# Up phase of a hybrid transformer layer: operand sums on VectorE alone, another priority scope, and the stores of u on ScalarE's queue

## The chip, the cores and the metric

The kernel runs on one core of one Trainium2 chip. The metric is the device time of one execution in microseconds. A core has five engines with an instruction queue each: PE (TensorE, matmuls), DVE (VectorE), ACT (ScalarE), POOL (GpSimd) and SP (SyncE, which here only issues DMAs). Each engine takes its instructions in order. ACT can issue DMAs as well. Matmul results go to PSUM, which has eight banks; DVE and ACT read them out of there.

## What is computed

The reference is one step of one layer for a prompt of 1024 rows and a sample of 8 x 16 rows, in fp32: an attention branch with a forget gate, a gated-delta branch, a merge of both, and a channel mixer. The change touches the channel mixer alone:

```
def channel_mixer(x, pre_g, post_g, w_up, w_down):
    h = rmsnorm(x, pre_g)
    u = jnp.square(jax.nn.relu(h @ w_up))
    return x + rmsnorm(u @ w_down, post_g)
```

`w_up` is 1024 x 4096 and `w_down` 4096 x 1024. Prompt and sample are worked on together: 1152 rows of h, nine tiles of 128.

## The kernel before

Each fp32 matmul is made of three: a value is split into a high and a low part (`split`, L325: ACT casts the high part, L326; DVE subtracts it to get the low part, L327), and high x high, high x low and low x high are added up in PSUM (`mm3`, L147, the matmul itself at L150). h lies transposed in SBUF as `hhi` and `hlo` (the profile calls them mhi and mlo in this phase).

The up phase (L1238 to L1360) computes u transposed, 32 row tiles of 128 features. Its first four row tiles are plain products (`gemm_t`, three groups of 384 columns each; `evu` does Relu and Square on ACT, L1280 and L1281, and stores to the DRAM tensor `u_d`, L1283). Beside them `h_sums` makes the operands `TT[0..3]` (th) from h: for each pair of column tiles two differences made by `diff` (x and y on POOL, L1252 and L1253, their sum on DVE, L1254), two by `rest` (both steps on DVE, L1259 and L1260), and a split of each into th. In all 20 POOL operations, 16 of 128x512 and 4 of 128x256.

The other 28 row tiles are done in 14 pairs by Winograd's form of Strassen's scheme: seven products in place of eight, each of sums of weight blocks with sums of h blocks. `w_ops` is a generator of the weight operands. For a pair it loads four blocks (`wr`, L1308, on SP), makes four sums (`add`, L1295, on POOL, tile `ws`) and splits the seven operands into `wh` and `wl`. The loop takes them three ahead (`ahead`). Each product has two column groups c, 320 and 256 wide, of 12 matmuls each, and each group takes one of eight PSUM banks in turn. Results are read out by ACT (product 0, a copy, L1357) or DVE (all others, `plus`, an addition to a running sum, L1347), into `s` tiles, of which there are 14 (and 4 `s1`). Four times a pair a row tile is finished in each column group: Relu (L1351), Square (L1352) and the store to `u_d` (L1353), eight stores a pair.

The down phase (from L1362) loads row tiles of u back (`ur`, L1400) and blocks of `w_down` (`raw`, L1406), both on SP, splits them into us and wd, and multiplies. A load of `gpost` (L1410) stands near its start in SP's queue.

The order of instructions in each queue is not the order of the code. A framework places them before the run, by the priority at which they were written (`tc.high_priority(n)` puts what is written inside its scope n places ahead) and by its model of costs. It also puts in the waits: a tile's buffer is reused when its readers are done, and each DMA signals on one of eight completion semaphores in turn, so that it first waits for the one before on the same semaphore. In `w_ops` the `yield` stands inside the scope of priority 50: while the generator rests there, the scope is still open, and what the consumer writes then (matmuls, evictions, stores) is written inside it.

Of the kernel before, what the change touches and what calls it, by code (L numbers as in the profile page):

```python
# [12 lines left out]
ALU = mybir.AluOpType  # L13
# [41 lines left out]
E0 = 4  # L55
XB = 1
LOW = 100000
HI = 200
KBB = 3
RB = 2  # L60
# [5 lines left out]
def tile_step(ctx, tc, x_prompt, x_sample, cache_k, cache_v, cache_logf, state_gdn, state_conv,  # L66
# [4 lines left out]
    V, A, G, S, T = nc.vector, nc.scalar, nc.gpsimd, nc.sync, nc.tensor  # L71
# [83 lines left out]
    hhi = ph.tile([P, NTT, KT, P], F32R, name="hhi")  # L155
    hlo = ph.tile([P, NTT, KT, P], F32R, name="hlo")
# [912 lines left out]
    with tc.tile_pool(name="fp", bufs=1, reuse_waits="tile") as fp:  # L1069
# [15 lines left out]
        for p in range(NP_):  # L1085
            q, k, v2, vn, qkn = nxt
            oT = fp.tile([P, NPR], F32, tag="oT", bufs=2, name=nm("oT"))
            for hh in range(2):
# [5 lines left out]
                for s in range(4):  # L1094
                    pr = fox_scores(fp, s, *qk)
# [14 lines left out]
    hhi = ph.tile([P, NTT, KT, P], F32R, name="mhi")  # L1110
    hlo = ph.tile([P, NTT, KT, P], F32R, name="mlo")
# [119 lines left out]
    u_d = dr.tile([DFF // P, P, 2, TH], F32, name="u_d")  # L1231
# [6 lines left out]
    with tc.tile_pool(name="up", bufs=1, reuse_waits="tile") as up:  # L1238
        def h_sums(t0, t1):

            n = t1 - t0

            def B(h, i, j):
                return f(h[:, t0:t1, 4 * i:4 * i + 4, 64 * j:64 * j + 64])

            def tmp():
                z = up.tile([P, 4, P], F32, tag="ws", bufs=4, name=nm("ws"))
                return z.rearrange("p k (t n) -> p (k t n)", t=2).rearrange("p (t k n) -> p t k n", t=2, k=4)[:, :n]

            def diff(a, b):  # L1250
                x, y = tmp(), tmp()
                G.tensor_tensor(x, B(hhi, *a), B(hhi, *b), ALU.subtract)  # L1252
                G.tensor_tensor(y, B(hlo, *a), B(hlo, *b), ALU.subtract)  # L1253
                V.tensor_tensor(x, x, y, ALU.add)  # L1254
                return x

            def rest(a, x):
                y = tmp()
                V.tensor_tensor(y, B(hhi, *a), x, ALU.subtract)  # L1259
                V.tensor_tensor(y, y, B(hlo, *a), ALU.add)  # L1260
                return y

            def out(i, x):
                split(x, *(z[:, :, 64 * t0:64 * t1].rearrange("p k (t n) -> p t k n", n=64) for z in TT[i]))
            t1_ = diff((0, 1), (0, 0))
            out(0, t1_)
            t2_ = rest((1, 1), t1_)
            out(1, t2_)
            out(2, diff((1, 1), (0, 1)))
            out(3, rest((1, 0), t2_))  # L1270

# [5 lines left out]
        for ft in range(N0):  # L1277
            def evu(c, acc, ft=ft):
                r, u = piece("s", 14, CH), piece("s", 14, CH)
                A.activation(r, acc, AF.Relu)  # L1280
                A.activation(u.rearrange("p (h t n) -> p t h n", h=2, n=64),  # L1281
                             r.rearrange("p (t h n) -> p t h n", h=2, n=64), AF.Square)
                S.dma_start(u_d[ft, :, :, 192 * c:192 * c + 192], u.rearrange("p (h n) -> p h n", h=2))  # L1283
            gemm_t(weights(halves(w_up[0], ft * P)), hhi, hlo, KT, evu, tag=("mm", NMM[0]))
            for t in ((0, 2), (4,), (6, 8), ())[ft]:
                h_sums(t, min(t + 2, NTT))
# [4 lines left out]
        def w_ops():  # L1291

            def add(x, y, op):
                z = up.tile([P, 4, P], F32, tag="ws", bufs=4, name=nm("ws"))
                G.tensor_tensor(z, x, y, op)  # L1295
                return z

            def parts(x):
                h, l = (wps_["w"].tile([P, 4, P], F32R, tag="w" + z, bufs=WBUFS["w"][1], name=nm("w" + z)) for z in "hl")
                split(x, h, l)  # L1300
                return h, l
            for pr in range(N0 // 2, DFF // P // 2):
                a = {}
                with tc.high_priority(200):
                    for i in range(2):
                        for j, src in enumerate(halves(w_up[0], (2 * pr + i) * P)):
                            a[i, j] = wps_["w"].tile([P, 4, P], F32, tag="wr", bufs=WBUFS["w"][0], name=nm("wr"))
                            S.dma_start(a[i, j], src.rearrange("(k p) n -> p k n", p=P))  # L1308
                with tc.high_priority(50):
                    yield parts(a[0, 0])  # L1310
                    s1 = add(a[1, 0], a[1, 1], ALU.add)
                    s2 = add(s1, a[0, 0], ALU.subtract)
                    yield parts(s2)
                    yield parts(add(a[0, 0], a[1, 0], ALU.subtract))
                    yield parts(a[1, 1])
                    yield parts(s1)
                    yield parts(a[0, 1])
                    yield parts(add(a[0, 1], s2, ALU.subtract))

        def hop(i, j):  # L1320
            return lambda k, t0, t1: [z[:, t0:t1, 4 * i + k, 64 * j:64 * j + 64] for z in (hhi, hlo)]
# [7 lines left out]
        for pr in range(N0 // 2, DFF // P // 2):  # L1329
            sm = [[], []]  # L1330
            for i, b in enumerate(prods):
                while len(ahead) < 3:
                    nx = next(made, None)
                    if nx is None:
                        break
                    ahead.append(nx)
                wh, wl = ahead.pop(0)
                for c, (t0, t1) in enumerate(GR):
                    n = 64 * (t1 - t0)
                    o = pt("mm", 8)[:, :n]  # L1340
                    mm3(o, [p3 for k in range(4) for hi, lo in (b(k, t0, t1),) for p3 in (
                        (wh[:, k], hi), (wh[:, k], lo), (wl[:, k], hi))])

                    def plus(x, r=None):
                        if r is None:
                            r = piece("s", 14, n)
                        V.tensor_tensor(r, o, x, ALU.add)  # L1347
                        return r

                    def done(row, half, r):  # L1350
                        A.activation(r, r, AF.Relu)  # L1351
                        A.activation(r, r, AF.Square)  # L1352
                        S.dma_start(u_d[2 * pr + row, :, half, 64 * t0:64 * t1], r)  # L1353
                    z = sm[c]
                    if i == 0:
                        r = piece("s1", 4, n)
                        A.copy(r, o)  # L1357
                        z.append(r)
                    elif i == 1:
                        z.append(plus(z[0]))  # L1360
                    elif i == 2:
                        z.append(plus(z[1]))  # L1362
                    elif i == 3:
                        done(1, 0, plus(z[2]))
                    elif i == 4:
                        plus(z[1], z[1])
                        done(1, 1, plus(z[2], z[2]))
                    elif i == 5:
                        done(0, 0, plus(z[0]))
                    else:  # L1370
                        done(0, 1, plus(z[1], z[1]))
# [22 lines left out]
    for blk in range(nb):  # L1394
        us, wd = uset[blk % 2], dset[blk % 2]
        for i in range(FB):
            ft = blk * FB + i
# [89 lines left out]
```

## Time and profile before

| | us |
|---|---|
| time, median of 3 runs | 2034.62 (2031.67 to 2039.93) |
| the profiled execution | 2027.51 |
| its span (first to last instruction) | 2025.7 |
| PE busy in 1200.0 to 1602.4 (end of the up phase's matmuls) | 390.98 of 402.40 |
| DVE, ACT, POOL busy there | 225.84, 193.16, 104.40 |
| PE busy from 1602.4 to the end (down phase) | 401.74 of 423.30 |

All times in the following are microseconds from the span's start, in the profiled execution. An engine's busy time counts only computing instructions; an idle stretch is followed by what ended it. A line such as L327 is a line of the kernel; a helper like `split` has the same line for every tile, so the tile's name tells which operation it is. `SPq` and `ACTq` are the queues in which these engines issue DMAs. The rows that the prediction rests on stand in it.

### The profile page before, as it was taken

What the parts mean: (1) busy time and instruction counts of PE and PEld (TensorE: products, weight loads), DVE (VectorE), ACT (ScalarE), POOL (GpSimd) and SP (SyncE); (2) the same over time, 40 slices, a digit from 0 to 9 for tenths busy, and PEclk for the clock granted to TensorE, in tenths of its full rate; (3) what the DMA queues carried; (4) which work ended last, traced back from release to release, by engine and by line L of the source; (5) the groups of instructions that cost most, each with busy time, mean ns of one, the idle gap of its engine ahead of it and who ended that gap; (6) DMA issues with size and microseconds to landing.
All of it is one profiled execution on the core that took longest, in us unless ns stands there. A gap on an engine that the chain in (4) does not pass through costs nothing.

```text
span 2025.7 us, 31077 instructions
## 1 busy us (share of the span) xinstructions
PE 1923.0 (95%) x11228; PEld 1725.9 (85%) x11228; DVE 1159.7 (57%) x2627; ACT 925.7 (46%) x2160; POOL 338.7 (17%) x433
## 2 busy tenths in 40 slices
PE   7989999898999999999989999899999799999998
PEld 6979898798898878778989789899999678888886
DVE  6357577775765476776644469745454444444437
ACT  5433474654737475665543444455454451111112
POOL 1141332513312200000012004422222000000000
PEclk9999999999999999999999999999999899999999
DMA  6142424224243543432643631333232452322203
GB/s 192 44 101 67 100 67 113 69 76 130 54 133 109 172 155 101 141 107 80 203 137 106 203 108 45 94 99 104 83 110 67 153 186 90 98 92 93 87 16 146
DMA packets 240310, 219.33 MB, mean 108 GB/s; under 512 B 53628, under 2 KB 213176, under 8 KB 240156
## 3 DMA queue, kind: packets, MB, share of 16 engines
q1 hardware_dynamic: 225888, 198.09, 33.1%
q10 hardware_dynamic: 14268, 19.25, 2.7%
q8 instruction: 89, 1.46, 0.3%
q14 instruction: 65, 0.53, 0.1%
HBM read 155.54 MB, written 61.74 MB: 107 GB/s over the span
## 4 chain that ended last, share of the span: by engine, by line
PE 75%; DVE 8%; DMA 7%; ACT 5%; issue 3%; POOL 2%; SPq 1%; DVEq 0%; POOLq 0%; ACTq 0%
PE mm L150 44%; PE mf L150 13%; PE pc L1011 2%; PE pa L150 1%; DMA be<-rows_o 1%; PE pc L150 1%; DVE th L327 1%; PE pe L150 1%; DVE xs L610 1%; DMA out_dram<-kst 1%; PE pb L150 1%; PE pd L150 1%; DMA wor<-in_w_out_dram 1%; PE mm L1040 1%; PE mm L1061 1%
## 5 line engine op out<-in xcount | busy, mean ns | idle before, releaser
L150 PE MATMUL mm<-wd,us 128*128 128x512 f32 x1728 | 401.7, 394 | 11.7 <-ACT wd L326 11.7
L150 PEld LDWEIGHTS mm<-wd,us 128*128 128x128 f32 x1728 | 325.7, 189 | 87.5 <-ACT wd L326 13.3
L150 PE MATMUL mf<-hhi,wlo 128*128 128x384 f32 x744 | 262.0, 352 | 3.2 <-DVE wlo L327 3.2
L150 PE MATMUL mf<-hhi,whi 128*128 128x384 f32 x744 | 260.9, 351 | 1.8 <-ACT gst L211 1.8
L150 PE MATMUL mf<-hlo,whi 128*128 128x384 f32 x744 | 261.4, 351 | 0.0
L150 PE MATMUL mm<-th,wh 128*128 128x256 f32 (+1 forms) x896 | 178.1, 295 | 4.5 <-ACT wh L326 3.6
L1435 DVE TENSOR_TENSOR yacc<-mm,yacc 128x512 f32<-128x512 f32 x126 | 86.2, 688 | 128.8 <-PE mm L150 128.6
L1347 DVE TENSOR_TENSOR s<-mm,s 128x320 f32<-128x320 f32 (+1 forms) x196 | 85.2, 454 | 108.3 <-PE mm L150 107.0
L150 PEld LDWEIGHTS mm<-th,wh 128*128 128x128 f32 x896 | 142.6, 189 | 5.1 <-ACT wh L326 3.8
L150 PEld LDWEIGHTS mf<-hhi,wlo 128*128 128x128 f32 x744 | 141.5, 190 | 4.4 <-DVE wlo L327 4.1
L150 PEld LDWEIGHTS mf<-hhi,whi 128*128 128x128 f32 x744 | 141.4, 190 | 2.4 <-ACT gst L211 2.1
L150 PEld LDWEIGHTS mf<-hlo,whi 128*128 128x128 f32 x744 | 141.3, 190 | 0.6
L150 PE MATMUL mm<-th,wl 128*128 128x320 f32 (+1 forms) x448 | 126.3, 296 | 0.7 <-DVE wl L327 0.7
L326 ACT CAST wd<-raw 128x512 fp32r<-128x512 f32 x64 | 38.3, 619 | 187.1 <-DVE yacc L1435 80.0
L327 DVE TENSOR_TENSOR wlo<-raw,whi 128x512 fp32r<-128x512 f32 x110 | 76.6, 698 | 69.5 <-ACT whi L326 68.7
L150 PE MATMUL mm<-mhi,wh 128*128 128x320 f32 (+1 forms) x336 | 100.5, 299 | 6.2 <-DVE s L1347 4.5
L150 PE MATMUL mm<-hhi,whi 128*128 128x384 f32 x288 | 103.7, 360 | 2.7 <-ACT whi L326 2.1
L150 PE MATMUL mm<-hhi,wlo 128*128 128x384 f32 x288 | 100.5, 349 | 2.1 <-DVE wlo L327 2.1
L150 PE MATMUL mm<-hlo,whi 128*128 128x384 f32 x288 | 101.9, 354 | 0.0
L326 ACT CAST whi<-raw 128x512 fp32r<-128x512 f32 x110 | 68.0, 619 | 68.1 <-PE mf L150 31.0
L150 PE MATMUL mm<-mhi,wl 128*128 128x320 f32 (+1 forms) x336 | 98.9, 294 | 0.0
L150 PE MATMUL mm<-mlo,wh 128*128 128x320 f32 (+1 forms) x336 | 98.9, 294 | 0.0
(494 smaller groups left out, 4343.5 us busy)
## 6 DMA issues: line engine op xcount, KB each, us to landing
raw<-in_w_in_dram SPq DMA_DIRECT2D x86, 256.0 KB
ur<-u_d SPq DMA_DIRECT2D x32, 576.0 KB
raw<-in_w_down_dram SPq DMA_DIRECT2D x64, 256.0 KB
wr<-in_w_up_dram SPq DMA_DIRECT2D x56, 256.0 KB
gate_d<-gst ACTq DMA_DIRECT2D x48, 192.0 KB
ga<-gate_d SPq DMA_DIRECT2D x48, 192.0 KB
u_d<-s SPq DMA_DIRECT2D x56, 160.0 KB
xt<-in_x_prompt_dram SPq DMA_DIRECT2D x16, 512.0 KB
```

The lines of the kernel that those rows point to most:

```text
L150: T.matmul(out, a, b, start=first and i == 0, stop=last and i == n - 1)
L326: A.copy(h, raw)
L327: V.tensor_tensor(l, raw, f(h), ALU.subtract)
L610: (A.copy if h else V.tensor_copy)(xs[0:64, h], st_[64 * h:64 * h + 64])
L1011: T.matmul(acc[:, q0:256], v2[:, 2 * jp + jj, P * hh:P * hh + P], q[:, jj * 256 + q0:jj * 256 + 256], start=jp == 0 and jj == 0 and k == 0 ...
L1040: T.matmul(a[32 * b:32 * b + 32, P:384], qbd[:, b].rearrange("p h t -> p (h t)"), kt, start=True, stop=True)
L1061: T.matmul(o[:, bs], vc[:, 2 * b + i], pT[:, 1 + i, bs], start=False, stop=b == 3 and i == 1)
L1347: V.tensor_tensor(r, o, x, ALU.add)
L1435: V.tensor_tensor(yacc[:, t, ns], acc, yacc[:, t, ns], ALU.add)
```

## The change

Three things are changed, in the up phase only. All lines behind them move: by 1 up to L1309 of the new numbering, by 5 behind `w_ops`.

```diff
+WPRIO = 60
...
             def diff(a, b):
                 x, y = tmp(), tmp()
-                G.tensor_tensor(x, B(hhi, *a), B(hhi, *b), ALU.subtract)
-                G.tensor_tensor(y, B(hlo, *a), B(hlo, *b), ALU.subtract)
+                V.tensor_tensor(x, B(hhi, *a), B(hhi, *b), ALU.subtract)
+                V.tensor_tensor(y, B(hlo, *a), B(hlo, *b), ALU.subtract)
                 V.tensor_tensor(x, x, y, ALU.add)
...
-                S.dma_start(u_d[ft, :, :, 192 * c:192 * c + 192], u.rearrange("p (h n) -> p h n", h=2))
+                A.dma_start(u_d[ft, :, :, 192 * c:192 * c + 192], u.rearrange("p (h n) -> p h n", h=2))
...
             def add(x, y, op):
                 z = up.tile([P, 4, P], F32, tag="ws", bufs=4, name=nm("ws"))
-                G.tensor_tensor(z, x, y, op)
+                V.tensor_tensor(z, x, y, op)
                 return z
...
-                with tc.high_priority(50):
-                    yield parts(a[0, 0])
-                    s1 = add(a[1, 0], a[1, 1], ALU.add)
-                    s2 = add(s1, a[0, 0], ALU.subtract)
-                    yield parts(s2)
...
+                def op(k):
+                    nonlocal s1, s2
+                    if k == 1:
+                        s1 = add(a[1, 0], a[1, 1], ALU.add)
+                        s2 = add(s1, a[0, 0], ALU.subtract)
+                    return parts(a[0, 0] if k == 0 else s2 if k == 1 else add(a[0, 0], a[1, 0], ALU.subtract) if k == 2 else
+                                 a[1, 1] if k == 3 else s1 if k == 4 else a[0, 1] if k == 5 else
+                                 add(a[0, 1], s2, ALU.subtract))
+                for k in range(7):
+                    with tc.high_priority(WPRIO):
+                        r = op(k)
+                    yield r
...
                     def done(row, half, r):
                         A.activation(r, r, AF.Relu)
                         A.activation(r, r, AF.Square)
-                        S.dma_start(u_d[2 * pr + row, :, half, 64 * t0:64 * t1], r)
+                        A.dma_start(u_d[2 * pr + row, :, half, 64 * t0:64 * t1], r)
```

First, the 20 sums of h and the 56 sums of weights go from POOL to DVE; POOL then has nothing in this phase. Second, the scope of priority (60 in place of 50) is closed before an operand is handed on, so that the consumer's work is written outside it. Third, the 124 stores of u (12 of L1283, 112 of L1353) are issued by ACT.

Before the up phase the order on every engine is the same. DVE, where `h_sums` begins, before (the name behind the arrow is read; ws tiles carry a number of their own):

```order
L1254 TENSOR_TENSOR ws_13347<-ws_13347,ws_13348 128x512
L1259 TENSOR_TENSOR ws_13354<-mhi,ws_13347 128x512
L1260 TENSOR_TENSOR ws_13354<-ws_13354,mlo 128x512
L327 TENSOR_TENSOR th_13235<-ws_13347,th_13234 128x2x4x64
L1254 TENSOR_TENSOR ws_13359<-ws_13359,ws_13360 128x512
L327 TENSOR_TENSOR th_13241<-ws_13354,th_13240 128x2x4x64
L1259 TENSOR_TENSOR ws_13366<-mhi,ws_13354 128x512
L327 TENSOR_TENSOR th_13239<-ws_13359,th_13238 128x2x4x64
```

The same place in the changed kernel:

```order
L1253 TENSOR_TENSOR ws_13347<-mhi 128x512
L1254 TENSOR_TENSOR ws_13348<-mlo 128x512
L1255 TENSOR_TENSOR ws_13347<-ws_13347,ws_13348 128x512
L1260 TENSOR_TENSOR ws_13354<-mhi,ws_13347 128x512
L1253 TENSOR_TENSOR ws_13359<-mhi 128x512
L1261 TENSOR_TENSOR ws_13354<-ws_13354,mlo 128x512
L328 TENSOR_TENSOR th_13235<-ws_13347,th_13234 128x2x4x64
L1254 TENSOR_TENSOR ws_13360<-mlo 128x512
L328 TENSOR_TENSOR th_13241<-ws_13354,th_13240 128x2x4x64
L1255 TENSOR_TENSOR ws_13359<-ws_13359,ws_13360 128x512
L1260 TENSOR_TENSOR ws_13366<-mhi,ws_13354 128x512
```

L1253 and L1254 have come in; the rest keeps its order. Up to the sum that the second product's weights need (ws_13791) DVE now has 75 instructions, 61 of 512 elements a partition and 14 of 256; before, DVE had 53 up to that operand's low part.

PE, in the product loop, at product 4 of the second pair: mm_14223 is its 320-wide group, mm_14241 its 256-wide one, mm_14271 the first group of product 5. Before:

```order
L150 MATMUL mm_14223<-th_13235,wh_14143 128x320
L150 MATMUL mm_14223<-th_13234,wl_14144 128x320
L150 MATMUL mm_14241<-th_13234,wh_14143 128x256
L150 MATMUL mm_14271<-mhi,wh_14177 128x320
L150 MATMUL mm_14271<-mlo,wh_14177 128x320
L150 MATMUL mm_14271<-mhi,wl_14178 128x320
```

and some 470 rows later, at product 4 of the fifth pair (mm_15069), with the groups of the third and fourth pair (mm_14517, mm_14793):

```order
L150 MATMUL mm_15051<-th_13234,wl_14972 128x320
L150 MATMUL mm_15069<-th_13234,wh_14971 128x256
L150 MATMUL mm_14793<-th_13235,wh_14695 128x256
L150 MATMUL mm_14241<-th_13235,wh_14143 128x256
L150 MATMUL mm_15069<-th_13235,wh_14971 128x256
L150 MATMUL mm_14517<-th_13235,wh_14419 128x256
L150 MATMUL mm_14793<-th_13234,wl_14696 128x256
```

The first of these two places in the changed kernel:

```order
L151 MATMUL mm_14223<-th_13235,wh_14143 128x320
L151 MATMUL mm_14223<-th_13234,wl_14144 128x320
L151 MATMUL mm_14241<-th_13234,wh_14143 128x256
L151 MATMUL mm_14241<-th_13235,wh_14143 128x256
L151 MATMUL mm_14241<-th_13234,wl_14144 128x256
L151 MATMUL mm_14241<-th_13234,wh_14143 128x256
L151 MATMUL mm_14241<-th_13235,wh_14143 128x256
L151 MATMUL mm_14241<-th_13234,wl_14144 128x256
```

Before, the 256-wide group is opened by one matmul and the eleven others are put off by three pairs; now its 12 matmuls stand together, as do those of all groups of the loop.

SP, from the end of the product loop into the down phase, before:

```order
L1353 DMA u_d<-s_17602 128x256
L1410 DMA gpost_17657<-in_norm_mlp_post_dram 128x1024
L1353 DMA u_d<-s_17438 128x320
L1353 DMA u_d<-s_17487 128x256
L1353 DMA u_d<-s_17453 128x256
L1400 DMA ur_17693<-u_d 128x1152
L1400 DMA ur_17705<-u_d 128x1152
L1406 DMA raw_17697<-in_w_down_dram 128x512
```

and in the changed kernel:

```order
L1309 DMA wr_17299<-in_w_up_dram 128x4x128
L1309 DMA wr_17301<-in_w_up_dram 128x4x128
L1415 DMA gpost_17657<-in_norm_mlp_post_dram 128x1024
L1405 DMA ur_17693<-u_d 128x1152
L1405 DMA ur_17705<-u_d 128x1152
L1411 DMA raw_17697<-in_w_down_dram 128x512
```

The stores have left the queue; they stand in ACT's, behind the Square that each of them needs. `gpost` waits for one of the last matmuls of the loop, in both kernels.

More of the change, by code (lines that the diff above doesn't have):

```diff
@@ L1308, in w_ops @@
                             S.dma_start(a[i, j], src.rearrange("(k p) n -> p k n", p=P))
-                with tc.high_priority(50):
-                    yield parts(a[0, 0])
-                    s1 = add(a[1, 0], a[1, 1], ALU.add)
-                    s2 = add(s1, a[0, 0], ALU.subtract)
-                    yield parts(s2)
[L1314 to L1318, printed above, removed]
+                s1 = s2 = None
+                def op(k):
[10 more added lines that the diff above has]
+                    yield r
         def hop(i, j):
```

## Prediction

> **What bounds the kernel now.** I read the page first, then the waits and the windows of the up phase, then the timelines at the places that these two name. The page shares the span out:
>
> ```profile
> PE 1923.0 (95%) x11228; PEld 1725.9 (85%) x11228; DVE 1159.7 (57%) x2627; ACT 925.7 (46%) x2160; POOL 338.7 (17%) x433
> ```
>
> TensorE is busy 95% of the time, and this change adds or removes no matmul. So only the 5% in which PE stands still can be won, and of it only the part in or right after the up phase. The waits of PE from 1200 to 1650 us (columns: total us, times, longest) name those gaps:
>
> ```profile
> PE mm L150 <- ACT wd L326: 11.7, 3, 10.3
> PE mm L150 <- DVE s L1347: 4.5, 3, 1.7
> PE mm L150 <- ACT wh L326: 3.6, 1, 3.6
> PE mm L150 <- ACT s L1357: 1.5, 3, 0.5
> PE mm L150 <- ACT s L1280: 0.9, 1, 0.9
> PE mm L150 <- DVE wl L327: 0.7, 1, 0.7
> ```
>
> That is 23 us in three places: the start of the product loop (wh, wl, s L1280), three stalls in it (s L1347 with s L1357), and the passage to the down phase (wd). The windows between the ends of these gaps show what each costs (length, then PE, PEld, DVE, ACT and POOL busy, the granted clock, DMA share, GB/s):
>
> ```profile
> 1274.39:1277.60 3.21, 3.21 (x25) 3.13 (x24) 3.17 (x6) 0.46 (x2) 1.42 (x3) 1.00 0.00 0
> 1277.60:1286.57 8.97, 3.73 (x14) 2.93 (x12) 8.16 (x9) 6.51 (x15) 7.00 (x6) 0.81 0.28 82
> 1286.57:1387.19 100.62, 100.62 (x756) 100.27 (x756) 48.74 (x88) 46.47 (x102) 25.27 (x19) 1.00 0.33 102
> 1393.27:1397.76 4.49, 2.30 (x15) 1.87 (x13) 4.49 (x6) 3.03 (x7) 2.57 (x3) 1.00 0.00 0
> 1485.46:1489.95 4.49, 2.30 (x16) 1.87 (x14) 4.49 (x6) 3.03 (x7) 2.56 (x3) 1.00 0.01 4
> 1577.65:1581.67 4.02, 2.32 (x15) 1.88 (x13) 4.02 (x9) 2.93 (x7) 0.00 (x0) 1.00 0.11 35
> 1602.40:1612.67 10.27, 0.00 (x0) 0.00 (x0) 2.98 (x5) 4.23 (x8) 0.00 (x0) 0.70 0.87 299
> ```
>
> One product (12 matmuls of 320, 12 of 256) takes 3.21 us where nothing is late, and its 320-wide half is the distance between these two rows, 1.76 us:
>
> ```profile
> 1274.39 0.31 PE L150 MATMUL mm<-mhi,wh 128*128 128x320 f32 x1
> 1276.15 0.28 PE L150 MATMUL mm<-mhi,wh 128*128 128x256 f32 x1
> ```
>
> From 1277.60 to 1286.57 PE does one such half, at a granted clock of 0.81: it loses 8.97 - 1.76 = **7.2 us**. Each of the three stall windows also holds one half: 2.73 + 2.73 + 2.26 = **7.7 us**. Between stalls PE is full for 100.62 us, while DVE and ACT are both under half busy.
>
> **Part 1, sums on DVE alone.** At the start of the product loop DVE is the late one, and it is late because its operations are long. The timelines of DVE and POOL (start, duration):
>
> ```profile
> 1239.44 0.68 DVE L327 TENSOR_TENSOR th<-ws,th 128x512 fp32r<-128x512 f32 x1
> 1239.67 1.61 POOL L1253 TENSOR_TENSOR ws<-mlo 128x512 f32<-128x512 f32 x1 [0.69 <-DVE ws L1259]
> 1240.05 1.78 DVE L1260 TENSOR_TENSOR ws<-ws,mlo 128x512 f32<-128x512 f32 x1
> 1248.17 0.68 DVE L1254 TENSOR_TENSOR ws<-ws,ws 128x512 f32<-128x512 f32 x1
> 1248.77 0.68 DVE L1259 TENSOR_TENSOR ws<-mhi,ws 128x512 f32<-128x512 f32 x1
> ```
>
> The same shape takes 0.68 us alone and starts 0.60 after the one before it, but 1.78 while a POOL operation runs beside it: each POOL operation of 1.6 us costs DVE 1.1. Without POOL the 22 operations that DVE now gets before the first weight sum that PE waits for are cheaper than the disturbance. DVE's order of the changed kernel has 75 instructions from the first of L1253 to that sum (ws_13791): 61 of 512 and 14 of 256 elements. The first position is the one of this row (today L1254); the second and third give the pace of the narrow ones, 0.33 to 0.34, and the fourth and fifth what an operation costs that needs the one just before, 0.72:
>
> ```profile
> 1277.03 0.42 DVE L1254 TENSOR_TENSOR ws<-ws,ws 128x256 f32<-128x256 f32 x1
> 1277.36 0.42 DVE L1259 TENSOR_TENSOR ws<-mhi,ws 128x256 f32<-128x256 f32 x1
> 1232.89 0.68 DVE L1254 TENSOR_TENSOR ws<-ws,ws 128x512 f32<-128x512 f32 x1
> 1233.61 0.69 DVE L1259 TENSOR_TENSOR ws<-mhi,ws 128x512 f32<-128x512 f32 x1
> ```
>
> (In time the last two rows come first: the start is 1232.89.) 61 x 0.60 + 14 x 0.34 = 41.4 us, and up to 17 dependent neighbours at 0.12 add 2.0, so the sum is there at 1274.3 to 1276.4. Today the chain that PE waits for is this:
>
> ```profile
> 1279.32 1.32 POOL L1295 TENSOR_TENSOR ws<-ws,wr 128x512 f32<-128x512 f32 x1 [0.42 <-POOL ws L1295]
> 1280.68 0.62 ACT L326 CAST wh<-ws 128x512 fp32r<-128x512 f32 x1 [1.85 <-POOL ws L1295]
> 1281.33 1.28 DVE L327 TENSOR_TENSOR wl<-ws,wh 128x512 fp32r<-128x512 f32 x1 [0.40 <-ACT wh L326]
> ```
>
> With the cast (0.62) and the split (0.68, behind two further sums, 1.2 us, that cover the cast) wh is ready at 1275.0 to 1277.0 and wl at 1276.3 to 1278.4; PE wants them at 1277.6 and 0.3 later. I leave 1.0 us of the loss for DVE waiting on casts that ACT now does behind store issues, so the gain is **6.2** (bounds 7.2, nothing left, and 3.5, half of the loss left).
>
> The Trainium skill, "VectorE: DVE Perf Modes", section "The DRAIN you can't avoid", speaks against this part: the next Vector operation does not start until the pipe of the one before is empty, and one should keep the count of operations down. By that rule each costs its full 0.68 or 0.42 and next to nothing of the 6.2 is left; that is rival 1. The rows at 1248.17 and 1248.77 do not bear it out: the second starts 0.08 before the first has ended.
>
> In the steady loop the 4 weight sums of a pair of row tiles (7 products, 22 us) come to DVE: over the window of 100.62 us POOL's 19 become 19 x 0.68 = 13 us, beside 48.74 now. DVE stays at 62 of 100, hidden under PE; three operands are made ahead, 9 us of cover.
>
> **Part 2, the scope.** Today the consumer's matmuls and evictions run inside the scope of whichever `yield` was open, and the order puts groups aside: mm_14241 is opened with one matmul, and its other eleven come 470 rows later, mixed with three groups of the next three pairs. Four of the eight PSUM banks finish together, and PE waits for DVE to empty one, then for ACT:
>
> ```profile
> 1395.25 0.39 PE L150 MATMUL mm<-mhi,wh 128*128 128x320 f32 x1 [1.67 <-DVE s L1347]
> 1397.76 0.38 PE L150 MATMUL mm<-mhi,wh 128*128 128x256 f32 x1 [0.52 <-ACT s L1357]
> ```
>
> In the changed order every group of the loop is 12 rows on end, so a bank comes back into use seven groups, some 11 us, after its last matmul, and its eviction takes 0.5. The three stalls go. What would be late next is an eviction behind a split on DVE, 1 us against those 11. I count **7.0** of the 7.7 (bounds 7.7 and 5.0).
>
> **Part 3, the stores.** On SP they wait for ACT in order, and loads wait behind them. Inside the loop no load is late for PE (no wait of PE above names a wr load), so nothing is won there. At its end it is:
>
> ```profile
> 1601.01 0.33 SPq L1410 DMA_DIRECT2D gpost<-in_norm_mlp_post_dram  x1
> 1601.43 3.66 SPq L1353 DMA_DIRECT2D u_d<-s  x3
> 1605.14 0.93 SPq L1400 DMA_DIRECT2D ur<-u_d  x2
> 1609.54 1.15 ACT L326 CAST us<-ur 128x1152 fp32r<-128x1152 f32 x1 [4.96 <-DMA ur<-u_d]
> 1612.67 1.74 PE L150 MATMUL mm<-wd,us 128*128 128x512 f32 x3 [10.28 <-ACT wd L326]
> ```
>
> The last matmuls end at 1602.40; the first ur load is issued 2.74 later, behind three stores, and the rest of the 10.28 is its landing, the casts and the raw loads. In the changed order it stands right behind gpost, which waits for the loop's last matmuls: about 0.4 after them. Gain **2.3** (bounds 3.7, if gpost goes out where it does now and ur at 1601.4, and 0). The landing stays.
>
> The Trainium skill, "DMA: Bandwidth & Descriptors", section "Issuing engines are not separate DMA queues", says that issuing on several engines saves only the issue time. By that rule 3 x 0.33, about 1 us, would be won here. Of the 3.66 us in the row most is SP waiting for ACT's s, which is not issue time.
>
> ACT pays with 8 store issues a pair. The same kind on ACT (gate_d) and its time in the whole trace:
>
> ```profile
> L212 ACTq DMA_DIRECT2D gate_d<-gst x48: 326/326/375, 573.3 to 1043.8; - x48
> ```
>
> 36 in the 100.62 us are 12 us at 0.33, or 14 at the longest, 0.375; with 46.47 that is 58 to 60 of 100.62. Hidden. Behind a waiting store on ACT stand casts of weights, needed 9 us later.
>
> **The sum**: 6.2 + 7.0 + 2.3 = 15.5 us off the profiled execution's 2027.5, which gives 2012.0. That execution lies 7.1 below the median of the runs shown; against the median, 2034.6 - 15.5 = **2019.1**.
>
> **Rivals.**
> 1. *DVE's chain is as late as before*, because its operations do not overlap: 61 x 0.68 + 14 x 0.42 = 47.4 us, the sum is there at 1280.3 and wh at 1280.9, against 1281.3 today. Part 1 gives 0.4: -9.7, 2024.9. For it: with x, y and their sum all on DVE more neighbours depend on each other, and casts of th stand on ACT behind stores. Against: the starts 0.60 apart in the timeline. The skill's rule on the DRAIN ends here.
> 2. *The passage is not shortened* because the first ur load waits for the last stores anyway: -13.2, 2021.4. For it: ur reads what the stores write. Against: the first ur load reads the first row tile, stored at the loop's start. The skill's rule on issuing engines ends near here, at -14.2.
> 3. *Slower: ACT is blocked by its own stores.* A store waits until the transfer before it on the same completion semaphore (eight in turn, loads and stores alike) has landed; behind it stand casts and the Relu that free buffers. A pair has 12 transfers, so eight are 22 x 8 / 12 = 15 us on average, some 10 where they bunch. The price decides at 10.2 + 15.5 = 26 us, or 1.9 us of PE wait in each of 14 pairs; at 2 us it is 28 - 15.5 = +12.5, 2047.1. Against: landings of ur take 5 us with the DMA share at 0.87, and the loop's share is 0.33.
> 4. *The stalls come back at another place* (the order alone shows no time): without the 7.0, -8.5, 2026.1. For it: all evictions still share DVE with splits and now sums.
>
> **How the numbers follow.** Chances: forecast 0.62, rival 1 0.14, rival 2 0.08, rival 3 0.10, rival 4 0.06. A difference within 0.5%, 10.2 us, is about what cannot be told from no change. The forecast (0.59 of its 0.62) and nearly all of rival 2 (0.07) lie beyond it: faster 0.66. Rivals 1 and 4 and the remainders make "same" 0.24; rival 3 is slower, 0.10. The range: the forecast's best bounds are 7.2 + 7.7 + 3.7 = 18.6 off, 2016.0, and 5 us more for the spread of a median (the three runs span 8.3), 2011; upward it takes in rivals 1 and 4 with a spread of 4: 2030. Rival 3 and tails stay out.
>
> **What would show it.** Right: from 1277 on PE has no wait above 1 us on ACT wh or DVE wl, DVE's 512-wide operations in the start stretch all take 0.68, no wait on DVE s L1352 in the loop, and ur is issued within 0.5 us of the last matmul. Wrong: DVE idle in the start stretch on ACT th (rival 1), stores on ACT waiting several us with casts behind (rival 3), new PE waits on s of 1 us or more at a regular distance (rival 4).

## The result, and the profile after

| | kernel before | changed kernel |
|---|---|---|
| time, median of 4 runs | 2033.7 (2031.67 to 2039.93) | 2012.74 (2010.57 to 2019.13) |
| ratio, with its 95% interval | | 0.9897 (0.9866 to 0.9928) |
| the profiled execution | 2027.5 | 2010.6 |
| its span | 2025.7 | 2008.9 |

The changed kernel is faster by 1.0%, some 21 us; the forecast was 15.5 us less and 2019.1, and the measured median lies near the lower end of its range, 2011 to 2030. The page of the changed kernel shows the same matmuls with less idle time around them, and POOL's work gone over to DVE:

```profile
PE 1921.8 (96%) x11228; PEld 1729.6 (86%) x11228; DVE 1180.3 (59%) x2703; ACT 927.5 (46%) x2160; POOL 234.5 (12%) x357
```

76 instructions have gone from POOL to DVE, 104 us there, and DVE is busy only 20.6 us longer, since its other operations became shorter. The waits of PE from 1200 to 1650 us (total us, times, longest) are these, and no others:

```profile
PE mm L151 <- ACT wd L327: 10.2, 1, 10.2
PE mm L151 <- DVE wd L328: 0.2, 1, 0.2
```

The waits on wh, wl and s are all gone; the one at the passage to the down phase is as long as it was. The windows (length, then PE, PEld, DVE, ACT, POOL busy, granted clock, DMA share, GB/s) cut the execution at the loop's first matmul, its end and the first matmul of the down phase, first before, then after:

```profile
1274.39:1602.40 328.01, 316.59 (x2353) 312.99 (x2352) 163.80 (x300) 159.63 (x356) 75.78 (x58) 0.99 0.29 92
1602.40:1612.67 10.27, 0.00 (x0) 0.00 (x0) 2.98 (x5) 4.23 (x8) 0.00 (x0) 0.70 0.87 299
1612.67:2025.70 413.03, 401.74 (x1728) 325.69 (x1728) 192.09 (x277) 92.75 (x140) 2.35 (x1) 0.99 0.31 105
```

```profile
1276.79:1586.50 309.71, 309.71 (x2353) 309.64 (x2352) 186.20 (x350) 157.06 (x349) 0.00 (x0) 1.00 0.31 96
1586.50:1596.82 10.32, 0.13 (x3) 0.01 (x1) 2.33 (x3) 3.98 (x7) 0.00 (x0) 0.62 0.88 294
1596.82:2008.90 412.08, 402.60 (x1728) 326.46 (x1728) 192.04 (x277) 92.76 (x140) 2.34 (x1) 0.98 0.32 105
```

So the loop of products is 18.3 us shorter, the passage not at all, the down phase 1.0. From the loop's start to the last instruction that is 19.2 us. The loop itself starts 2.4 us later, at 1276.79 and not 1274.39, though the order of the work ahead of it is the same; in the 14 profiles of this study that start lies anywhere from 1273 to 1289. Below, therefore, stretches from the loop's start on are compared, and whole times only where runs were timed in rounds.

### The profile page after: what moved, and what is told of

Same layout as the page of the kernel before. It is cut to its first block, busy times and chain, and to the rows that moved or that the text cites. A ratio compares the mean times of both kernels' runs of the same rounds, so it can differ in the third digit from the quotient of the medians.

```text
span 2008.9 us, 30893 instructions
## 1 busy us (share of the span) xinstructions
PE 1921.8 (96%) x11228; PEld 1729.6 (86%) x11228; DVE 1180.3 (59%) x2703; ACT 927.5 (46%) x2160; POOL 234.5 (12%) x357
## 4 chain that ended last, share of the span: by engine, by line
PE 78%; DMA 7%; DVE 6%; ACT 4%; issue 3%; POOL 1%; SPq 1%; DVEq 0%; ACTq 0%; POOLq 0%
PE mm L151 46%; PE mf L151 13%; PE pc L1012 2%; DMA wor<-in_w_out_dram 1%; PE pc L151 1%; PE pe L151 1%; PE pa L151 1%; DMA out_dram<-kst 1%; PE pb L151 1%; PE pd L151 1%; DVE xs L611 1%; PE pa L454 1%; PE mm L1041 1%; PE mm L1062 1%; PE pb L1003 1%
## 5 line engine op out<-in xcount | busy, mean ns | idle before, releaser
L151 PE MATMUL mm<-wd,us 128*128 128x512 f32 x1728 | 402.6, 395 | 10.5 <-ACT wd L327 10.2
L151 PE MATMUL mm<-th,wl 128*128 128x320 f32 x448 | 131.4, 293 | 0.0
```

The lines of the kernel that those rows point to most:

```text
L151: T.matmul(out, a, b, start=first and i == 0, stop=last and i == n - 1)
```

## The experiments

One table for all of them, from the profiles: the loop (first matmul of product 0 to the last of the loop, both ends taken alike in every run), PE's first wait at the passage, and what lies between the loop's end and the last instruction. Where the passage is the same (changed, e10_after, e5_no_sums, e8_h_pool, e9_w_pool) the last column still scatters from 422.2 to 424.1, with later waits on wd of up to 2.2 us.

| kernel | loop | wait at the passage | from the loop's end on |
|---|---|---|---|
| before | 327.8 | 10.4 | 423.5 |
| changed | 309.7 | 10.3 | 422.4 |
| sums alone (e1_sums) | 320.2 | 10.6 | 422.3 |
| scope alone (e2_scope) | 320.0 | 10.0 | 421.8 |
| stores alone (e3_stores) | 331.3 | 9.1 | 420.3 |
| changed without the sums (e5_no_sums) | 320.8 | 10.4 | 424.1 |
| changed without the scope (e6_no_scope) | 320.1 | 9.0 | 420.0 |
| changed without the stores (e7_no_stores) | 311.0 | 9.8 | 422.1 |
| changed, sums of h on POOL (e8_h_pool) | 320.1 | 10.2 | 422.6 |
| changed, sums of weights on POOL (e9_w_pool) | 310.5 | 10.2 | 422.2 |
| changed, gpost late (e4_gpost_late, e11_gpost_late) | 311.0, 311.0 | 4.8, 4.8 | 418.8, 418.2 |
| changed again (e10_after) | 310.0 | 10.3 | 422.6 |
| stores on SP, gpost late (e12_sp_gpost_late) | 309.7 | 9.7 | 420.8 |

Seven of these kernels have one time each, which holds the scatter of the loop's start too: 2021.1, 2023.0 and 2029.9 us for the sums, the scope and the stores alone, 2025.1 without the sums, 2025.8 without the scope, 2018.2 and 2015.4 with the sums of h and of weights on POOL.

### One part at a time

The sums alone, on the kernel before:

```diff
-                G.tensor_tensor(x, B(hhi, *a), B(hhi, *b), ALU.subtract)
-                G.tensor_tensor(y, B(hlo, *a), B(hlo, *b), ALU.subtract)
+                V.tensor_tensor(x, B(hhi, *a), B(hhi, *b), ALU.subtract)
+                V.tensor_tensor(y, B(hlo, *a), B(hlo, *b), ALU.subtract)
...
-                G.tensor_tensor(z, x, y, op)
+                V.tensor_tensor(z, x, y, op)
```

> Only the sums go to DVE (20 of h, 56 of weights); scope and stores as before. The loop of products lasted 328.0 us before (first matmul of product 0 to the last of the loop) and 309.7 after. If the loss at the loop's start comes from POOL slowing DVE, it goes by itself here: PE waits on wh and wl at the start fall from 4.3 to under 1 us, the three stalls on s stay (about 6 us of waits), and the loop lasts about 321. Rival: the start was late because of the scope's order; then the waits on wh stay and the loop lasts about 328. On the 3.4 us of the loop's gain that neither the start (7.2) nor the stalls (7.7) explain: if they come from the scope, the pace between stalls stays at 3.195 us a product here; if they come from POOL being silent, it falls to 3.16 here.

Measured: 320.2, with no wait of PE at the start and the stalls at every fourth pair still there. The start's loss was the sums. The second question is answered by the scope's run.

The scope alone, on the kernel before (`op` as in the diff of the change):

```diff
-                with tc.high_priority(50):
-                    yield parts(a[0, 0])
...
+                for k in range(7):
+                    with tc.high_priority(WPRIO):
+                        r = op(k)
+                    yield r
```

> Only the scope is changed; sums on POOL and stores on SP as before. If the held-back column groups cause the stalls, no wait on s is left in the loop, the start keeps its loss of about 7 us, and the pace is 3.16 us a product: the loop lasts about 317. Rival for the 3.4 us: if they come from POOL being silent, the pace stays at 3.195 and the loop lasts about 320.5. Rival for the stalls: if they come from DVE being slowed by POOL, three waits on s of 1.5 us stay.

Measured: 320.0, between the two values and for a reason that neither had: no wait on s of the stalls in the loop, but a costlier start. (The scope's two changes, the earlier close and 60 in place of 50, were not run apart.) What the scope removes is seen in the distance between two first copies of a pair (ACT, L1357 or L1362, the copy of product 0; start, duration). In the kernel before:

```profile
1368.63 0.43 ACT L1357 COPY s<-mm 128x320 f32<-128x320 f32 x1 [1.17 <-PE mm L150]
1397.28 0.43 ACT L1357 COPY s<-mm 128x320 f32<-128x320 f32 x1 [1.28 <-PE mm L150]
1418.98 0.42 ACT L1357 COPY s<-mm 128x320 f32<-128x320 f32 x1 [1.17 <-PE mm L150]
1439.90 0.43 ACT L1357 COPY s<-mm 128x320 f32<-128x320 f32 x1 [1.16 <-PE mm L150]
1460.82 0.43 ACT L1357 COPY s<-mm 128x320 f32<-128x320 f32 x1 [1.16 <-PE mm L150]
```

and with the scope alone:

```profile
1380.21 0.43 ACT L1362 COPY s<-mm 128x320 f32<-128x320 f32 x1 [0.38 <-PE mm L151]
1402.33 0.43 ACT L1362 COPY s<-mm 128x320 f32<-128x320 f32 x1 [0.38 <-PE mm L151]
1424.45 0.43 ACT L1362 COPY s<-mm 128x320 f32<-128x320 f32 x1 [0.38 <-PE mm L151]
```

Before, four pairs take 1460.82 - 1368.63 = 92.2 us, three short ones (part of their work is put off) and one of 28.65; with the scope each takes 22.12, four 88.5. A stall thus costs 3.7 us, not the 2.7 that the window at its end showed; the run without scope has the same 28.5 beside DVE sums. Of the 1.0 between them, 0.7 is in the burst ahead of the wait. Four times in a burst PE goes over from put-off groups to the running product, and there its first matmul takes 0.22 us to the next one's start, some 0.1 more than the rest, and the one before it 0.04 to 0.19 more. One such place in the kernel before:

```profile
1389.81 0.38 PE L150 MATMUL mm<-mhi,wh 128*128 128x256 f32 x1
1390.03 0.28 PE L150 MATMUL mm<-mlo,wh 128*128 128x256 f32 x1
1390.15 0.28 PE L150 MATMUL mm<-mhi,wl 128*128 128x256 f32 x1
```

The other 0.3 is pace: between the stalls a 320-wide and a 256-wide matmul together take 264.4 ns in the kernel before and 263.3 in the changed one, which is 22.21 and 22.12 us a pair. Why is open; the same two paces come back below without a change of scope.

POOL's silence has no part in the pace: with POOL working (scope alone) pairs are at 22.12 too. The rival for the 3.4 us falls.

That the start costs 10 us here and 7.2 in the profile before lies in the granted clock. In the kernel before, and then with the scope alone (same columns as in the windows above, cut on a grid of 3.41 us, on which the clock changes in these traces):

```profile
1278.86:1282.27 3.41, 0.56 (x2) 0.30 (x2) 3.01 (x4) 1.11 (x3) 2.78 (x3) 1.00 0.18 58
1282.27:1285.69 3.42, 3.03 (x10) 2.63 (x10) 3.01 (x5) 3.36 (x8) 2.16 (x2) 0.50 0.52 153
1285.69:1289.10 3.41, 2.53 (x20) 2.53 (x20) 3.41 (x3) 3.06 (x7) 3.33 (x3) 1.00 0.63 194
```

```profile
1283.55:1286.97 3.42, 0.00 (x0) 0.00 (x0) 3.24 (x4) 1.54 (x4) 3.00 (x3) 1.00 0.18 58
1286.97:1290.38 3.41, 2.76 (x9) 2.36 (x10) 3.19 (x4) 2.89 (x7) 2.40 (x2) 0.50 0.35 100
1290.38:1293.79 3.41, 2.53 (x11) 2.13 (x10) 2.99 (x3) 3.35 (x9) 2.72 (x3) 0.50 0.62 189
1293.79:1297.21 3.42, 3.42 (x16) 3.42 (x15) 3.42 (x5) 0.88 (x2) 2.73 (x3) 0.50 0.21 66
```

Some 4 us after PE falls idle the clock is halved; in the profile before it was halved for one such window, 3.4 us, here for three, 10.2. In the other late starts it was three windows too (stores alone, h on POOL) or four, 13.7 us (without the sums). The profile of before, at 2027.5 us faster than every timed run of its kernel, had the cheapest late start of the five.

The stores alone, on the kernel before, in `evu` and `done`:

```diff
-                S.dma_start(u_d[ft, :, :, 192 * c:192 * c + 192], u.rearrange("p (h n) -> p h n", h=2))
+                A.dma_start(u_d[ft, :, :, 192 * c:192 * c + 192], u.rearrange("p (h n) -> p h n", h=2))
...
-                        S.dma_start(u_d[2 * pr + row, :, half, 64 * t0:64 * t1], r)
+                        A.dma_start(u_d[2 * pr + row, :, half, 64 * t0:64 * t1], r)
```

> Only the stores go to ACT; sums and scope as before. The loop should stay at 328 us (within 1), since no load was late. The first ur load is issued under 1 us after the last matmul instead of 2.7. If the landing takes back what the earlier issue gains, PE stands still about 10 us at the passage as in both kernels; if the earlier issue counts, 8. Rival that ACT is blocked by its stores: the loop gets longer by several us.

Measured: the loop is 3.5 us longer, where at most 1 was expected, and the passage and what follows 3.2 shorter, so nothing on balance. PE's waits at the start (1270 to 1300) show 1.4 of the first:

```profile
PE mm L150 <- ACT wh L326: 3.7, 1, 3.7
PE mm L150 <- ACT s L1280: 2.3, 1, 2.3
PE mm L150 <- DVE wl L327: 0.8, 2, 0.5
```

The wait on s (L1280) was 0.9 and is 2.3: the Relu that frees a PSUM bank now stands behind store issues of 0.52 us and the Square that each waits for. The other 2 us fit the longer halved clock (10.2 us in place of 3.4). So a store on ACT does delay what is queued behind it, where that is wanted at once, and not elsewhere. With the sums on DVE the same stores cost nothing, as the next runs show.

### Leaving one part out

Each of these is the changed kernel with one of the three diffs above turned round. Without the sums:

> The changed kernel with the sums back on POOL (scope and stores as changed). In the run with the scope alone the loop lasted 320.0 us, 10.3 more than in the changed kernel, all of it at the start. If that is the sums, this loop lasts about 320 too, with PE waits on wh and wl of 4 us or more at the start and pairs of 22.12 us after it. If the stores on ACT make the start later still (casts behind them), it lasts 322 to 324.

Measured: 320.8, pairs of 22.12 after a late start, as expected, and the wait on s at the start is 2.3 here too.

Without the scope:

> The changed kernel with the scope of before (sums and stores as changed). The loop should last about 320, as with the sums alone (320.2): no wait at the start, every fourth pair 28.5 us in place of 22.1. At the passage gpost waits for a matmul that this order has 1.2 us before the end, as in the kernel before and in the run with the stores alone; if gpost is what ur waits behind, PE stands still about 9 us (9.1 there) and not 10.3.

Measured: 320.1 and a wait of 9.0 at the passage, as expected. So in the company of the others the scope is worth 10.4 us of the loop and the sums 11.1; alone they gave 7.8 and 7.6. That does not show that the two losses overlap: the gains of one part alone are taken against the profile of before, whose late start cost 7.2 us, where a late start cost 10 to 11 in the runs with the scope alone, without the sums and with h on POOL. With a start of that price in the kernel before (its loop was 331.3 with the stores alone), the parts alone would come out some 3 us higher, as they do in company.

Which of the sums it is: in the changed kernel first those of h go back to POOL (the first two lines of the sums' diff turned round), then those of weights instead:

```diff
-                V.tensor_tensor(z, x, y, op)
+                G.tensor_tensor(z, x, y, op)
```

> The changed kernel with the 20 sums of h back on POOL, the 56 of weights on DVE. If POOL's operations stretch DVE's in the start stretch (1.7 to 1.8 us in place of 0.7), most of the loss at the start is back: the loop lasts 315 to 320. If what counted was the sum of weights at the chain's end (two POOL operations of 1.3 us in a row), it lasts about 311 to 313.

> The changed kernel with the 56 sums of weights back on POOL, those of h on DVE. If the loss at the start is POOL's h sums beside DVE, the loop lasts 310 to 313 (the first weight sums on POOL cost at most 2 x 1.35 us and stretch two or three DVE operations). In the steady loop DVE's splits get longer (0.75 to 0.8 in place of 0.69) without any wait of PE, so pairs stay at 22.12. If it is the weight sums, the loop lasts 315 or more.

Measured: 320.1 and 310.5. It is the 20 sums of h. The groups of DVE in the changed kernel, from 1230 to 1280 (busy us, mean ns), and then the same 16 and 8 operations with h on POOL (window 1218 to 1592):

```profile
L328 DVE TENSOR_TENSOR th<-ws,th 128x512 fp32r<-128x512 f32 x16 | 10.8, 685 | 0.4 <-ACT th L327 0.3
L1261 DVE TENSOR_TENSOR ws<-ws,mlo 128x512 f32<-128x512 f32 x8 | 5.5, 684 | 0.0
```

```profile
L328 DVE TENSOR_TENSOR th<-ws,th 128x512 fp32r<-128x512 f32 x16 | 19.3, 1229 | 0.0
L1261 DVE TENSOR_TENSOR ws<-ws,mlo 128x512 f32<-128x512 f32 x8 | 10.3, 1284 | 0.0
```

The same operations take 1.23 and 1.28 us beside POOL and 0.68 without. The 56 weight sums on POOL stretch DVE's splits too (0.72 to 0.76 us against 0.69), but in the steady loop nobody waits for them: pairs stay at 22.12, and the start has one wait of 0.6. Their move is worth 0.5 to 0.8 us, by the two profiles of the changed kernel (310.0 and 309.7).

### The passage

Here the forecast of 2.3 us failed: SP issued as it said, and PE waited as before. SP's DMA issues and ACT's first casts in the changed kernel:

```profile
1586.54 0.34 SPq L1415 DMA_DIRECT2D gpost<-in_norm_mlp_post_dram  x1
1586.94 0.90 SPq L1405 DMA_DIRECT2D ur<-u_d  x2
```

```profile
1593.40 1.15 ACT L327 CAST us<-ur 128x1152 fp32r<-128x1152 f32 x1 [5.37 <-DMA ur<-u_d]
1595.09 1.15 ACT L327 CAST us<-ur 128x1152 fp32r<-128x1152 f32 x1 [0.54 <-DMA ur<-u_d]
```

ur is issued 0.45 us after the last matmul and not 2.7, but from the issue to its cast it now takes 6.5 us, and before it took 4.4 (1605.14 to 1609.54). Two things had come nearer to it: gpost, 512 KB, which goes out 0.4 us ahead of ur and went out 4.1 ahead before, and ACT's last stores. The packets in the traces tell the two apart. With nothing close in front, ur's first packet starts 1.0 to 1.1 us after its issue (kernel before, sums alone, and the three runs with gpost late, also where stores go out 0.4 us ahead of ur). In all seven runs in which gpost goes out 0.4 us ahead it starts 3.2 to 3.8 us after, as gpost's 128 packets of 4 KB come to their end (1.05 to 4.45 us after the loop's end in the changed kernel; ur's first at 4.03). With gpost 1.8 us ahead (scope alone, without the stores' move) it is 1.7. The long delay holds too in the two runs in which ACT's last two stores are issued only 2.9 us behind ur (stores alone, without the scope). In the kernel before gpost's packets were through 0.6 us before ur was issued. So the longer landing comes in the main from gpost's transfer. And gpost holds up SP's queue itself; the longest of SP's waits in the changed kernel from 1570 to 1600 is this:

```profile
SPq L1415 <- PE mm L151: 20.2, 1, 20.2
```

So gpost was taken out of the passage:

```diff
         if last:
+            V.tensor_tensor(gpost[:, 0:1], yacc[:, 0, 0:1], yacc[:, 0, 1:2], ALU.add)
             S.dma_start(gpost, g_mlp_post[0].partition_broadcast(P))
```

> The changed kernel, but the load of gpost (512 KB) is made to wait for a one-column sum of yacc (written into gpost's first column and then overwritten by the load), so that it leaves the passage from the up to the down phase. In the changed kernel it is issued 0.4 us ahead of the first ur load, in the kernel before 4.1 us ahead. If gpost takes the DMA engines from ur, ur lands about 2 us sooner (4.3 instead of 6.4 us from issue to cast) and PE's wait at the passage falls from 10.2 to about 8. If it is ACT's last two stores that do, or a fixed latency, the wait stays within 0.5 us of 10.2. Time against the changed kernel: about 2 us less, or the same.

> The changed kernel with gpost's load made to wait for a sum of yacc, again, timed beside the changed kernel. In its first run ur was issued 7 us before the loop's last matmul and PE's waits at the passage were 6.6 us in place of 10.4; from the loop's end to the last instruction it was 418.8 in place of 422.4. Expected: 3 to 4 us (0.2%) under the changed kernel; ratio to the kernel before 0.988 to 0.990. If the gain at the passage is given back in the down phase, the two are the same.

Measured: more than expected at the passage. The wait falls from 10.3 to 4.8 in both runs, and the expectation had counted only the smaller reason, gpost's transfer. The larger is its place: its wait for the last matmul held SP's queue. SP and PE without it (e11_gpost_late; the last matmul starts at 1584.09):

```profile
1576.84 1.50 SPq L1405 DMA_DIRECT2D ur<-u_d  x2
1584.54 0.83 SPq L1411 DMA_DIRECT2D raw<-in_w_down_dram  x2
```

```profile
1589.00 0.70 PE L151 MATMUL mm<-wd,us 128*128 128x512 f32 x1 [4.64 <-ACT wd L327]
1590.70 13.67 PE L151 MATMUL mm<-wd,us 128*128 128x512 f32 x48 [1.00 <-ACT wd L327]
1605.78 29.53 PE L151 MATMUL mm<-wd,us 128*128 128x512 f32 x129 [1.40 <-ACT wd L327]
```

ur needs nothing from the last products; it goes out 7 us before the loop ends, and has landed when ACT is done with the loop's last Square. What PE waits for then is ACT's casts of us and wd, and raw. Two later waits of 1.0 and 1.4 give some of it back: from the loop's end on 418.2 and 418.8 against 422.4. Against that the loop lasts 311.0 in both runs of this kernel, its pairs 22.21 us in place of 22.12; the matmuls are the same, and why they run 0.4% slower stays open (the run without the stores' move has it too, and the kernel before between its stalls; the run with stores on SP and gpost late has not). In times, all but the last row beside the same runs of the kernel before (2035.28):

| | median | ratio to before |
|---|---|---|
| changed kernel (e10_after) | 2008.86 | 0.9866 (0.9852 to 0.9881) |
| gpost late (e11_gpost_late) | 2005.99 | 0.9853 (0.9837 to 0.9869) |
| changed without the stores (e7_no_stores) | 2012.11 | 0.989 (0.9857 to 0.9923) |
| stores on SP, gpost late (e12_sp_gpost_late) | 2012.19 | 0.9881 (0.9854 to 0.9907) |
| gpost late, first run (e4_gpost_late), before at 2032.99 | 2009.7 | 0.9875 (0.9855 to 0.9895) |

Gpost late is the fastest version tried, ahead by 3 us in the medians; the intervals of all rows overlap, so that the times alone do not tell them apart. Its ratio lies below the expected 0.988 to 0.990, as that of the changed kernel beside it lies below what was expected of it:

> The changed kernel again, unaltered, timed beside the next run on the same chip. From loop start to end the changed kernel's profile was 19.2 us shorter than that of before; its medians differed by 21 us, with starts of the loop that differ from run to run by some us. Expected ratio to the kernel before 0.990 to 0.9915.

Measured: 26 us below before in the same rounds, a larger gain than expected; its loop is 310.0.

What the stores are worth, with and without gpost in front of ur (`A.dma_start` back to `S.dma_start`; the second with the diff above):

> The changed kernel with the stores back on SP (sums and scope as changed). If the stores were never in anyone's way in the loop, it lasts 309.7 as in the changed kernel. At the passage gpost waits for the last matmul, two stores follow, and ur is issued 1.9 us after the last matmul in place of 0.45; in the run with the scope alone PE stood still 10.0 us that way. So the wait is 10.0 to 10.4 here too, and moving the stores is worth nothing while gpost is in front of ur. If the earlier issue of ur counts, it is 11.5 to 12.

> The stores on SP and gpost's load made late (sums and scope as changed). If, with gpost out of the way, the stores on SP are what ur waits behind, ur is issued 1.5 to 2.5 us after the last matmul, lands 4.4 later, and PE stands still 7 to 9 us, against 4.6 (6.6 with later waits) when ACT issues the stores; so the move of the stores is worth about 2 to 3 us here. If not, 4.6 here too.

Measured: 9.8 at the passage without the stores' move, 10.3 with it: worth nothing while gpost is in front. (The loop's 311.0, not the expected 309.7, is again pairs of 22.21.) With gpost late and the stores on SP the wait is 9.7, over the 7 to 9 expected: SP stands at its stores until 1.9 us after the last matmul.

```profile
1585.69 3.47 SPq L1358 DMA_DIRECT2D u_d<-s  x3
1589.25 0.88 SPq L1405 DMA_DIRECT2D ur<-u_d  x2
```

From the loop's end on it is 420.8 there, and 418.2 to 418.8 with the stores on ACT: 2.0 to 2.6 us for the move, which the changed kernel does not collect because of gpost. The first wait, 9.7 against 4.8, is clear; the 2.0 to 2.6 are hardly more than the scatter of that column. Here ur takes 4.6 us from issue to cast, with stores just ahead of it and no gpost.

## Why the prediction was right, and where it was not

**Part 1, the sums: right in mechanism, a little small.** DVE's chain was forecast at 41.4 to 43.4 us from its first sum to the second product's weight sum. In the changed kernel it is this, 42.9:

```profile
1235.30 0.68 DVE L1253 TENSOR_TENSOR ws<-mhi 128x512 f32<-128x512 f32 x1
1277.54 0.69 DVE L1296 TENSOR_TENSOR ws<-ws,wr 128x512 f32<-128x512 f32 x1
1279.34 1.29 DVE L328 TENSOR_TENSOR wl<-ws,wh 128x512 fp32r<-128x512 f32 x2
```

wl is there at 1280.0, some 0.2 us before PE wants it: just in time. The 1.0 us kept back for casts behind stores was hardly needed (DVE waited 0.4 us for casts in this stretch); the whole 7.2 came, 7.6 by the run with the sums alone. The 7.2 itself was read from the late start with the shortest halved clock; in other profiles the same flaw cost 10 to 11. Of the 60 distances between 512-wide operations of DVE in this chain 53 are 0.60 or 0.61, and those behind a result just made 0.72, so rival 1 is refuted, and with it the rule that the prediction took from the Trainium skill on the DRAIN, at least for such operations.

**Part 2, the scope: right in mechanism, too small.** The three stalls went with the held-back groups, which the runs with and without the scope show. The term "7.0 of the 7.7" was mis-sized: it took the stall for the window after the burst, and left out the burst itself (0.7 us a cycle) and the slightly slower pace (0.3). Measured by the pair's period a cycle costs 3.7 us, three of them (the last 3.2) 10.7, and 10.4 is what leaving the scope out costs. Rival 4 did not come true.

**Part 3, the stores: wrong.** ur went out 0.45 us after the last matmul, as said; the step that failed is "The landing stays". It grew by 2.1, since gpost's 512 KB, which had been through before ur was issued, now went out right in front of it, and PE's wait stayed at 10.3. The sign that was set for this part, ur issued within 0.5 us, came true all the same: it looked at the issue and not at PE's wait. Part 2 had a hand in this: in the old order gpost waited for a matmul 1.2 us before the end, in the new one for the last. With the old order the stores take 1.3 to 1.6 us off PE's wait and 2.3 to 3.2 off the stretch from the loop's end on (stores alone against before, without the scope against the sums alone), with the new one nothing. That gpost itself was the thing to move was not seen; bounds were put on its time of issue, and its 512 KB were not counted. Rival 2 gave the right outcome for the passage, by another mechanism.

**Rival 3** has a small true core: at a late start, stores on ACT made PE wait 1.4 us more. In the loop they cost nothing.

**The sum.** 6.2 + 7.0 + 2.3 = 15.5 stands against 18.3 + 0 + 1.0 = 19.2 in the profiles from the loop's start on, and against 21 and 26 in the two sets of timed runs. That the total came this near is in part luck: the loop gave 5.1 more than its 13.2, and the passage 2.3 less than its part. The profiled execution of before was shorter than the timed ones, partly for the clock at its start; so gains worked out against it came out low: with a late start of 10 to 11 us in place of 7.2 the 19.2 would be 22 to 23, an estimate from the other four late starts. How much of the difference between 19 and 26 is that, and how much the spread of the work before the loop, is not settled.

## What to carry to other kernels

An idle second engine is not free help: what POOL did in 1.6 us cost DVE 1.1 where DVE was the late one, and 56 more operations off the critical path cost next to nothing. A stall is to be measured by the period of the loop, not by the wait at its end. And before a queue is cleared of what stands in front of an urgent load, look at everything in front of it: here one load that nobody needs for hundreds of us, and that waits for the last matmul and then moves 512 KB, hid the gain.

## What the runs showed of the hardware

In the five late starts PE's clock was halved 2 to 5 us after PE fell idle, for 3.4 us in one run, 10.2 in three and 13.7 in one, at nearly the same first waits of 3.2 to 3.9 us. Within each run these changes lie on one grid of 3.41 us, placed differently in each run. The clock fell after windows of that grid in which PE had been busy for 0 to 1.44 us of the 3.41, and came back after the first one with 3.03 or more; windows with up to 2.88 left it halved. Elsewhere in the traces it also fell after windows with more work in them, so that this is not the whole rule. A late operand thus cost from 7 to 11 us, by how its waits fell on the grid. The Trainium skill, "TensorE: Matmul & The Clock Gate", section "Part 1: The HAM clock gate", describes this: after an idle window of about 3.4 us the clock is at half, after a busy one of the same length it is full, and the window runs freely, so that the number of slow matmuls differs from run to run. The traces agree on the length and on the free run; the window ahead of a fall was not always idle (1.44 us of work in the run without the sums).

A DVE operation with two inputs in SBUF that meets a POOL operation waits for it: 1.78 us in the kernel before, where POOL's had begun 0.4 earlier and took 1.6. In all 13 such meetings of 512-wide operations ahead of the loop, in the kernel before, DVE's ended 0.55 us after POOL's (0.56 in one). The Trainium skill, "SBUF — State Buffer", section "Who interferes with whom", says that the later of the two blocks until the first is done; the rows fit, since 1.61 - 0.38 of POOL's were left and 0.60 is DVE's own pace, 1.8 in all.
